# Hybrid attention and RWKV-7 layer: y products in the U half of a PSUM bank, four banks in turn, first RWKV step in the groups list

## The chip, the cores and the metric

The kernel runs on one core of a Trainium2 chip. The metric is device microseconds of one execution. The engines are named as in the profile: PE (TensorE matmul), PEld (its weight loads), DVE (VectorE), ACT (ScalarE), POOL (GpSimd) and SP (SyncE, which here only issues DMAs).

## What is computed

One transformer-like layer on 2048 latent tokens and 256 context tokens of width 1024. The reference, cut to the token mixer, which the change touches:

```python
q_l, k_l, v_l, rw_l = jnp.split(h_lat @ w_in, ATT_CUTS, axis=-1)
...
att_l = lax.map(lambda qb: gqa_attend(qb, k_all, v_all), q_blocks)      # 8 query heads, 2304 keys
...
for d, reverse in enumerate((False, True)):                              # RWKV-7, both directions, 8 heads
    s_c, yc = wkv7_scan(r_c, dc, kc, vr_c, ac, bc, s0, reverse, with_ctx_out)
    _, yl = wkv7_scan(r_l, dl, kl, vr_l, al, bl, s_c, reverse, True)
    y_l = yl if y_l is None else y_l + yl
rw_out_l = rwkv_output(y_l, r_l, kb_l, vr_l, g_l, r_k, lnx_g, lnx_b).astype(h_lat.dtype)
out_l = jnp.concatenate([att_l, rw_out_l], axis=-1) @ w_out
```

where one step of the scan is `S_t = S_{t-1} (diag(w_t) + a_t b_t^T) + v_t k_t^T ; y_t = S_t r_t`. Behind it come the output projection, a norm, and sixteen experts that each take their top 256 tokens.

## The kernel before

The layer runs in stages, one after the other: input projection (`inproj`), mixers (`mixers`), output projection (`outproj`), experts (`experts`). Only `mixers` is changed.

**Two kinds of work on one PE.** Attention runs in 32 units (a pair of heads by 256 queries), each of 9 groups of two key tiles. A group is four score matmuls (L871, L872) into tile `st`, two exponentials on ACT (L876) into `pt`, eight value matmuls (L897) into `po`, and two additions of `pt` to `acc` on POOL (L904) for the denominator. Ahead of a unit its queries are transposed (L823) and 20 products (L841) are each reduced to row maxima on DVE (L843). RWKV runs in 18 steps `m` (two pairs of heads, each a context step and 8 latent steps of 256 tokens, both directions at once). A step has these parts, each a generator: `elementwise` (the decay and rate products L1036, then a long run on ACT, DVE and POOL up to the tiles `AR` and `BK`), `lmats` and `trans` (products in chunks of 64, L1080, L1110, L1117), `inverse` (16x16 triangular inverses on DVE, sent through DRAM), `merges` (L1186), `chain` and, for the later half of a pair's steps, `post`.

**The chain** is the serial part: four quarters `c` per step, each carrying the state `S` on. A quarter does, in this order: 32 matmuls into `pa[:, 0]` (L1232, L1234), a copy to `xs` (L1237), 16 matmuls into `pa[:, 1]` (L1242, the U product), its two copies into `UV` (L1244), 16 matmuls back into `pa[:, 0]` (L1250), and, in a latent step, 32 y products (L1257, L1260). Then DVE forms `sn = pa[:, 0] + S` (L1263) and the new `S` (L1265), ACT copies `S` to `SB` (L1269), and y goes to `yt` by two ACT copies (L1274, first four latent steps of a pair) or two DVE additions (L1276, the last four). Tile `pa` (named `cha`) is 128x512 float32, a whole PSUM bank, and there is one of it. The y products have a bank of their own, tile `chy`.

**PSUM** has eight banks: three taken in turn under the name `bk` for everything else (each `bank()` call waits until the tile three calls back has been read), two for `st`, one each for `po`, `cha` and `chy`.

**Order on PE.** All matmuls of the mixers are put in one fixed order by `weave`, while the program is built. Each generator yields steps with a due time, a PE mode, a PE cost, the work that must follow (`seq`), work that nobody waits for (`bg`), what it needs, and how many `bk` banks it takes. `weave` keeps modelled clocks of PE, ACT, DVE and POOL and a list of when banks come free, and takes the step with the smallest key:

```python
key = due * self.STEP_NS + 30.0 * wait + cost      # STEP_NS = 66e3, cost 5000 where the PE mode changes
```

A step with mode `None` has no PE work and doesn't move the model's PE clock. PE then executes strictly in that order; the other engines' queues are ordered by the framework's scheduler.

**Before the list.** `first()` of attention (transposed keys, unit 0's queries and maxima) and `first()` of RWKV run ahead of `weave`. RWKV's `first()` loads the weights of two head pairs and then does `elementwise(0, i, 0)` and `lmats(0, i, 0)` for both `i`; the streams `elementwises` and `lmatss` start with step 1 and only name step 0 as made. The tile `wl` in pool `rwpre` exists once, and the raw weights (`headw`), the `wl` loads (L1023) and the tile `kd` of `elementwise` all take it in turn.

Of the kernel before, what the change touches and what calls it, by code (L numbers as in the profile page):

```python
# [10 lines left out]
F32 = mybir.dt.float32  # L11
# [24 lines left out]
class Layer:  # L36
# [614 lines left out]
    @staticmethod  # L651
    def step(due, mode=None, pe=0, seq=(), bg=(), need=(), bk=0):

        return due, mode, pe, seq, bg, need, bk
# [3 lines left out]
    def weave(self, streams):  # L660


        t = dict(PE=0.0, ACT=0.0, DVE=0.0, POOL=0.0)
        made, banks, shape = {}, [0.0] * 3, None

        def run(at, work):
            ends = []
            for e, ns in work:
                if e == "dma":
                    at += ns  # L670
                else:
                    t[e] = max(t[e], t["PE"]) + ns
                    at = max(t[e], at + ns + 100)
                ends.append(at)
            return at, ends

        live = []

        def forward(s):

            for x in s["gen"]:
                if isinstance(x, str):
                    late = x.endswith("+")
                    made[x.rstrip("+")] = max(s["ready"], t["POOL"] + 100) if late else s["ready"]
                else:
                    s["next"] = x
                    return
            live.remove(s)

        for g in streams:  # L690
            s = dict(gen=g, ready=0.0)
            live.append(s)
        for s in live[:]:
            forward(s)
        while live:
            best = None
            for s in live:
                due, mode, pe, seq, bg, need, bk = s["next"]
                if any(n not in made for n in need):
                    continue  # L700
                at = max([s["ready"]] + [made[n] for n in need] + banks[:bk])
                if mode is None:
                    wait, cost = max(at - t["PE"], 0.0), 0.0
                else:
                    wait, cost = max(at - t["PE"], 0.0), 0.0 if mode == shape else 5000.0
                key = due * self.STEP_NS + 30.0 * wait + cost
                if best is None or key < best[0]:
                    best = key, s, at
            _, s, at = best
            due, mode, pe, seq, bg, need, bk = s["next"]  # L710
            if mode is None:
                end = at = max(at, t["PE"])
                end, ends = run(at, seq)
            else:
                t["PE"] = max(t["PE"], at) + (0 if mode == shape else 170) + pe
                shape = mode
                end, ends = run(t["PE"] + 150, seq)
                if bk:
                    del banks[:bk]
                    banks += [ends[min(bk, len(ends)) - 1] if ends else end] * bk  # L720
            s["ready"] = end
            run(t["PE"], bg)
            forward(s)
# [16 lines left out]
    def attention(self, pools, pp):  # L740


        tc, nc = self.tc, self.nc
# [10 lines left out]
        step = self.step  # L754
# [5 lines left out]
            return RW * n / (NU * NG)  # L760

        def bank():
            return pp.tile([128, 512], F32, name="bk", bufs=3)

        def kprep(j, both):

# [171 lines left out]
    def rwkv(self, pools, pp):  # L938


        tc, nc, I = self.tc, self.nc, self.I
        CD = math.exp(-0.5)
        NB = 4
        NW = T // 256
        low, res, pre, lms, wk = (pools[n] for n in ("rwlow", "rwres", "rwpre", "rwlm", "rwwork"))
        ident = self.ident
        step = self.step
# [1 line left out]
        mean, hmean, gd, td, ypart = self.mean, self.hmean, self.gd, self.td, self.ypart  # L949

        def bank(shape):
            return pp.tile(shape, F32, name="bk", bufs=3)

        UPS, GW = {}, {}

        def headw(hp):
            hs = slice(128 * hp, 128 * hp + 128)
            raw = pre.tile([128, 2, 2, 256], F32, name="wl")[:, :, :, 0:128]
            for x, n in enumerate(("decay_up", "iclr_up")):
                for h in range(2):  # L960
                    nc.sync.dma_start(raw[cr(h), x], I[n][0, :, :, hs].rearrange("d k n -> k d n"))
            ups = UPS[hp] = [res.tile([128, 2, 2, 128], F32R, name=f"ups{a}", bufs=2) for a in range(2)]
            self.split(ups[0], ups[1], raw)
# [11 lines left out]
        def mats(t, h):  # L975

            return bass.AP(tensor=t.tensor, offset=t.offset + h * 8 * 4160, ap=[[64, 64], [4160, 8], [1, 64]])

        def cr(h):

            return slice(64 * h, 64 * h + 64)

        def tr(h):

            return slice(64 - 64 * h, 128 - 64 * h)
# [9 lines left out]
        N = len(steps)  # L995
        W, J, G, ST = {}, {}, {}, {}

        SB = [res.tile([128, 2, 2, 2, 64], F32, name=f"SB{j}") for j in range(2)]
        NS = [0]

        def hp_of(m, i):
            return 2 * steps[m][0] + i
# [70 lines left out]
        def products(m, i, x):  # L1073

            AR, BK = J[m]["AR"][:, i], G[m, i]["BK"]
            ps = [bank([128, 8, 64]) for _ in range(2)]
            for c in range(8):
                for h in range(2):
                    lhs = BK[cr(h), c].rearrange("p s j -> p (s j)")[:, 64 * h:64 * h + 128]
                    nc.tensor.matmul(ps[h][:, c], lhs, AR[cr(h), c, x], start=True, stop=True)  # L1080
            L = lms.tile([128, 8, 2, 64], F32, name="LR" if x else "LA", bufs=2 if x else 4)
            for h in range(2):
                nc.vector.tensor_mul(L[:, :, h], ps[h],
                                     mask[:, 64 * x:64 * x + 64].unsqueeze(1).to_broadcast([128, 8, 64]))
            return L

        def lmats(m, i, d0):
            yield step(d0, "r", 900, [("DVE", 687), ("DVE", 687)], bk=2, need=[f"E{m}.{i}"])
            LA = G[m, i]["LA"] = products(m, i, 0)
            for h in range(2):  # L1090
                nc.sync.dma_start(mats(gd[(2 * m + i) % NB], h), LA[tr(h), :, h])
            yield f"L{m}.{i}"
# [111 lines left out]
        def chain(m, d0):  # L1204
            pair, s = steps[m]
            lat = s >= 0
            yt = None
            for c in range(4):
                d1 = d0 + c * 0.1
# [14 lines left out]
                                                  .rearrange("i p n -> p i n"))  # L1224
                S = ST[0]
                pa = pp.tile([128, 2, 2, 2, 64], F32, name="cha", bufs=1)
                py = pp.tile([128, 2, 2, 64], F32, name="chy", bufs=1)
                for i in range(2):
                    for d in range(2):
                        q = 4 * d + c  # L1230
# [11 lines left out]
                            nc.tensor.matmul(pa[tr(h), 1, i, d], Y[i][tr(h), 4 * d + c], xs[tr(h), i, d], start=True, stop=True)  # L1242
                for h in range(2):
                    nc.scalar.copy(UV[tr(h), :, c::4, h], pa[tr(h), 1])  # L1244
                yield step(d1 + 0.06, "c", 1300 if lat else 430, [("DVE", 420), ("DVE", 420)],
                           [("ACT", 1150)] if lat else [])
                for i in range(2):
                    for d in range(2):
                        for h in range(2):
# [13 lines left out]
                nc.vector.tensor_add(sn, pa[:, 0], S)  # L1263
                ST[0] = wk.tile([128, 2, 2, 64], F32, name="S", bufs=2)
                nc.vector.tensor_mul(ST[0], sn, P[:, :, c::4].unsqueeze(3).to_broadcast([128, 2, 2, 64]))  # L1265
                if lat or c == 3:
                    NS[0] += 1
                    for h in range(2):
                        nc.scalar.copy(SB[NS[0] % 2][cr(h), h], ST[0][cr(h)])  # L1269
                if lat:  # L1270
                    for d in range(2):
                        dst = (yt[:, :, 1][:, :, ::-1] if d else yt[:, :, 0])[:, :, c * 64:(c + 1) * 64]
                        if s < NW // 2:
                            nc.scalar.copy(dst, py[:, :, d])  # L1274
                        else:
                            nc.vector.tensor_add(dst, py[:, :, d], dst)  # L1276
            if lat and s < NW // 2:
                for d, w in enumerate((s, NW - 1 - s)):
                    nc.sync.dma_start(ypart[2 * pair:2 * pair + 2, :, w * 256:w * 256 + 256].rearrange("i p n -> p i n"),
                                      yt[:, :, d])  # L1280
# [86 lines left out]
        def first():  # L1367
            for b in SB:
                nc.gpsimd.memset(b, 0.0)
            for i in range(2):  # L1370
                headw(i)
                load(0, i)
            for i in range(2):
                yield from elementwise(0, i, 0)
                yield from lmats(0, i, 0)


        OFF = 0.5

        def elementwises():  # L1380
            yield "E0.0"
            yield "E0.1"
            for m in range(1, N):
                for i in range(2):
                    yield from elementwise(m, i, m - 1.5 + OFF + 0.15 * i)
                    if m + 1 < N and steps[m + 1][1] < 0:
                        headw(hp_of(m + 1, i))

        def lmatss():
            yield "L0.0"  # L1390
            yield "L0.1"
            for m in range(1, N):
                for i in range(2):
                    yield from lmats(m, i, m - 1.25 + OFF + 0.15 * i)

# [705 lines left out]
```

## Time and profile before

| | |
|---|---|
| Time, median of 3 runs | 3928.14 us (3928.07 to 3928.42) |
| The profiled execution's own time | 3935.49 us |
| Its span | 3933.8 us |
| PE busy | 3555.9 us, 90% of the span |
| DVE, ACT, POOL busy | 66%, 44%, 37% |
| Mean granted TensorE clock | 0.944 of full speed |
| Mixers, about 669 to 2445 us | PE busy 1542.95 of the 1700 us from 740 to 2440 |

The busy time of PE is pipelined matmul time at whatever clock was granted, so a stretch at half clock looks busier than it is productive. An idle time in a row names what ended it, which for a tile taken in turn can be an instruction that the waiting one does not read.

### The profile page before, as it was taken

The numbers are of one execution on the slowest core, as the hardware profiler recorded it, in microseconds if no ns is written. First come the engines' busy times: TensorE is split into PE (matmuls) and PEld (weight loads), VectorE is DVE, ScalarE is ACT, GpSimd is POOL, SyncE is SP. The second block draws the span as 40 slices with busy tenths as digits, with TensorE's granted clock in tenths as the row PEclk, the third lists the DMA queues.
The fourth block names the chain that finished last, engine by engine and source line by source line (L and its number), as shares of the span: only waits on it lengthen the run. The fifth ranks groups of instructions, "written<-read, shape, count | busy, mean of one in ns | idle before, by whom it ended". The sixth has DMA issues, their size and how long they took to land. (4 is left out here: it accounts for less than half of the span.)

```text
span 3933.8 us, 83032 instructions
## 1 busy us (share of the span) xinstructions
PE 3555.9 (90%) x34103; PEld 2979.2 (76%) x34103; DVE 2603.1 (66%) x4413; ACT 1718.9 (44%) x3255; POOL 1445.9 (37%) x1326
## 2 busy tenths in 40 slices
PE   7999898699998988999998898993999999999986
PEld 6888897566666666666666666993999999999976
DVE  5665655567666776766666776787555556655688
ACT  4544353344444433444444434552444444444443
POOL 3332312456655554566655542333101101011025
PEclk8999999799999998999999998996999999999998
DMA  7756443223332323332232323434566667666675
GB/s 235 235 186 191 144 153 133 71 57 75 71 81 64 81 82 84 101 86 76 65 75 74 96 56 124 151 140 135 186 211 208 216 201 214 211 210 215 206 270 171
DMA packets 635533, 554.78 MB, mean 141 GB/s; under 512 B 264112, under 2 KB 584144, under 8 KB 635152
## 3 DMA queue, kind: packets, MB, share of 16 engines
q1 hardware_dynamic: 622672, 505.94, 41.9%
q0 software_dynamic: 12480, 43.52, 4.7%
q8 instruction: 268, 4.39, 0.4%
q14 instruction: 113, 0.93, 0.1%
HBM read 428.28 MB, written 121.03 MB: 140 GB/s over the span
## 5 line engine op out<-in xcount | busy, mean ns | idle before, releaser
L904 POOL TENSOR_TENSOR acc<-acc,pt 128x512 f32<-128x512 f32 x496 | 661.7, 1334 | 386.4 <-ACT pt L876 361.3
L48 DVE TENSOR_TENSOR wl<-wf,wh 128x1024 fp32r<-128x1024 f32 x434 | 532.7, 1253 | 264.3 <-ACT wh L43 264.3
L1979 PE MATMUL gu<-xh,wl 128*128 128x256 f32 x2048 | 584.6, 286 | 21.9 <-DVE wl L48 21.9
L1979 PE MATMUL gu<-xl,wh 128*128 128x256 f32 x2048 | 583.0, 285 | 0.0
L1979 PE MATMUL gu<-xh,wh 128*128 128x256 f32 x2048 | 581.8, 284 | 0.0
L43 ACT CAST wh<-wf 128x1024 fp32r<-128x1024 f32 x434 | 440.7, 1047 | 317.6 <-issue 106.1
L843 DVE TENSOR_REDUCE mx<-bk 128x1 f32<-128x512 f32 (+1 forms) x640 | 378.1, 629 | 183.7 <-PE bk L841 182.6
L876 ACT ACTIVATE pt<-st 128x512 f32<-128x512 f32 x576 | 317.1, 596 | 388.6 <-PE st L872 358.2
L1979 PEld LDWEIGHTS gu<-xh,wl 128*128 128x128 f32 x2048 | 390.3, 191 | 23.7 <-DVE wl L48 23.7
L1979 PEld LDWEIGHTS gu<-xh,wh 128*128 128x128 f32 x2048 | 391.3, 191 | 0.6
L1979 PEld LDWEIGHTS gu<-xl,wh 128*128 128x128 f32 x2048 | 389.4, 190 | 0.6
L897 PE MATMUL po<-pt,vt 128*64 128x256 f32 x2304 | 329.0, 412 | 0.9 <-ACT pt L876 0.9
L2023 POOL DMA_INDIRECT acc<-ysb,idx x30 | 48.3, 1611 | 675.0 <-DVE ysb L2020 589.3
L460 PE MATMUL mm<-hTh,wh 128*128 128x256 f32 x968 | 281.5, 291 | 4.4 <-POOL raw L479 2.2
L460 PE MATMUL mm<-hTl,wh 128*128 128x256 f32 x968 | 278.8, 288 | 1.2 <-DVE hTl L48 1.2
L460 PE MATMUL mm<-hTh,wl 128*128 128x256 f32 x968 | 276.2, 285 | 0.0
L841 PE MATMUL bk<-k,qs 128*128 128x512 f32 (+1 forms) x640 | 235.1, 436 | 37.3 <-DVE mx L843 23.2
L871 PE MATMUL st<-qs,k 128*128 128x512 f32 x576 | 253.8, 441 | 2.1 <-ACT pt L876 1.1
L872 PE MATMUL st<-q,kl 65*128 65x512 f32 x576 | 240.2, 417 | 12.9 <-DMA q<-mr 12.9
L897 PEld LDWEIGHTS po<-pt,vt 128*64 128x64 f32 x2304 | 150.1, 144 | 111.8 <-issue 59.8
L460 PEld LDWEIGHTS mm<-hTh,wh 128*128 128x128 f32 x968 | 186.5, 193 | 12.8 <-issue 7.9
L841 PEld LDWEIGHTS bk<-k,qs 128*128 128x128 f32 x640 | 108.6, 195 | 111.6 <-DVE mx L843 37.9
(431 smaller groups left out, 8401.4 us busy)
## 6 DMA issues: line engine op xcount, KB each, us to landing
wf<-in_exp_w_gate_dram SPq DMA_DIRECT2D x64, 1024.0 KB
wf<-in_exp_w_up_dram SPq DMA_DIRECT2D x64, 1024.0 KB
wf<-in_exp_w_down_dram SPq DMA_DIRECT2D x64, 1024.0 KB
win<-rkl SPq DMA_DIRECT2D x64, 512.0 KB
wf<-in_w_in_dram SPq DMA_DIRECT2D x30, 1024.0 KB
wf<-in_w_ada_dram SPq DMA_DIRECT2D x20, 1024.0 KB
wl<-wll SPq DMA_DIRECT2D x64, 256.0 KB
pwin<-rkl SPq DMA_DIRECT2D x32, 384.0 KB
```

Source lines behind the costliest of these rows:

```text
L43: nc.scalar.copy(hi, src)
L48: nc.vector.tensor_sub(lo, src, hi)
L460: mm = nc.tensor.matmul(ps[:, c], a[:, k, cs], b[:, k], start=m == 0, stop=m == 3 * KD - 1)
L841: nc.tensor.matmul(ps[:, :n], qs[:, hh, i * 128:(i + 1) * 128], K2[j][:, c * 512:c * 512 + n], start=True, stop=True)
L843: nc.vector.reduce_max(mx[:, hh * 2 + i, c:c + 1], ps[:, :n], axis=AX.X)
L871: nc.tensor.matmul(st, K2[j][:, ksl], qs, start=True, stop=False)
L872: nc.tensor.matmul(st, KL[j][:, ksl], q2, start=False, stop=True)
L876: nc.scalar.activation(pt, st, AF.Exp, scale=0.125)
L897: nc.tensor.matmul(po[hh * 64:(hh + 1) * 64], VT[j][:, kt], pt[:, hh], start=kt == 0, stop=kt == KT - 1)
L904: add(acc, acc, pt)
L1979: mm = nc.tensor.matmul(ps[:, i], a[:, k, 128 * c:128 * c + 128], b[:, k], start=n == 0, stop=n == 3 * KD - 1)
L2023: nc.gpsimd.indirect_dma_start(out=self.acc, in_=y[h], in_offset=None, compute_op=ALU.add, out_offset=bass.IndirectOffsetOnAxis(ap=idx[h], ...
```

## The change

Four edits, all in `mixers`. The y products go into `pa[:, 1]`, where U stood, and tile `chy` is gone. `bk` tiles are taken four in turn instead of three, in the kernel and in the planner's model. The planner's step for the last third of a quarter now counts y's two evictions as work that must follow (on ACT or DVE), and their place in the program moves ahead of the `SB` copies. And `first()` of RWKV ends after its loads (`return` ahead of a `yield`, so it stays a generator): `elementwise(0, i)` and `lmats(0, i)` are now in the streams, with the due times that the formulas give for m = 0.

```diff
-        made, banks, shape = {}, [0.0] * 3, None
+        made, banks, shape = {}, [0.0] * 4, None
...
-            return pp.tile([128, 512], F32, name="bk", bufs=3)
+            return pp.tile([128, 512], F32, name="bk", bufs=4)
...
-            return pp.tile(shape, F32, name="bk", bufs=3)
+            return pp.tile(shape, F32, name="bk", bufs=4)
...
                 pa = pp.tile([128, 2, 2, 2, 64], F32, name="cha", bufs=1)
-                py = pp.tile([128, 2, 2, 64], F32, name="chy", bufs=1)
+                py = pa[:, 1]
...
-                yield step(d1 + 0.06, "c", 1300 if lat else 430, [("DVE", 420), ("DVE", 420)],
-                           [("ACT", 1150)] if lat else [])
+                yield step(d1 + 0.06, "c", 1300 if lat else 430,
+                           [("DVE", 420), ("DVE", 420)] + [("ACT" if s < NW // 2 else "DVE", 300)] * (2 if lat else 0),
+                           [("ACT", 560)] if lat else [])
...
-                if lat or c == 3:
-                    NS[0] += 1
-                    for h in range(2):
-                        nc.scalar.copy(SB[NS[0] % 2][cr(h), h], ST[0][cr(h)])
                 if lat:
                     for d in range(2):
                         dst = (yt[:, :, 1][:, :, ::-1] if d else yt[:, :, 0])[:, :, c * 64:(c + 1) * 64]
...
                             nc.vector.tensor_add(dst, py[:, :, d], dst)
+                if lat or c == 3:
+                    NS[0] += 1
+                    for h in range(2):
+                        nc.scalar.copy(SB[NS[0] % 2][cr(h), h], ST[0][cr(h)])
...
-            for i in range(2):
-                yield from elementwise(0, i, 0)
-                yield from lmats(0, i, 0)
+            return
+            yield
...
         def elementwises():
-            yield "E0.0"
-            yield "E0.1"
-            for m in range(1, N):
+            for m in range(N):
                 for i in range(2):
                     yield from elementwise(m, i, m - 1.5 + OFF + 0.15 * i)
...
         def lmatss():
-            yield "L0.0"
-            yield "L0.1"
-            for m in range(1, N):
+            for m in range(N):
                 for i in range(2):
                     yield from lmats(m, i, m - 1.25 + OFF + 0.15 * i)
```

## Rows read from the trace of the kernel before

**Rows 1.** The page: busy time of PE, and the granted clock in 40 slices.

```profile
PE 3555.9 (90%) x34103; PEld 2979.2 (76%) x34103; DVE 2603.1 (66%) x4413; ACT 1718.9 (44%) x3255; POOL 1445.9 (37%) x1326
...
PEclk8999999799999998999999998996999999999998
```

**Rows 2.** Stretches: length, busy PE, PEld, DVE, ACT, POOL, granted clock, DMA share, GB/s.

```profile
680.00:700.00 20.00, 6.26 (x42) 5.81 (x42) 7.62 (x7) 3.44 (x7) 6.02 (x7) 0.50 0.30 98
700.00:720.00 20.00, 10.66 (x69) 8.18 (x68) 8.51 (x10) 5.88 (x13) 4.63 (x5) 0.50 0.30 63
...
740.00:2440.00 1700.00, 1542.95 (x18917) 1108.32 (x18919) 1152.43 (x2011) 731.42 (x1617) 937.22 (x781) 0.94 0.31 77
```

**Rows 3.** Timeline of PE, 669 to 717: start, length, instruction, idle before and what ended it.

```profile
684.11 2.05 PE L1036 MATMUL bk<-wl,ups 128*128 128x256 f32 x8 [13.84 <-DMA wl<-wlc]
695.05 3.68 PE L1080 MATMUL bk<-AR,BK 64*128 64x64 f32 x32 [8.89 <-DVE BK L1066]
699.46 2.26 PE L1036 MATMUL bk<-wl,ups 128*128 128x256 f32 x8 [0.74 <-DMA wl<-wlc]
710.78 3.77 PE L1080 MATMUL bk<-AR,BK 64*128 64x64 f32 x32 [9.06 <-DVE BK L1066]
```

**Rows 4.** Timeline of POOL in the same stretch, step 0, head pair 0.

```profile
687.84 1.71 POOL L1061 TENSOR_TENSOR wl<-wl,win 128x512 f32<-128x512 f32 x1 [3.82 <-DVE wl L1058]
...
691.50 1.18 POOL L1059 TENSOR_TENSOR AR<-win,P 128x512 f32<-128x512 f32 x1
...
692.94 1.42 POOL L1067 TENSOR_TENSOR BK<-wl,tw 64x512 f32<-64x512 f32 x1
```

**Rows 5.** Waits of PE, 740 to 2440: us in total, times, longest us.

```profile
PE bk L841 <- DVE mx L843: 19.8, 21, 2.0
...
PE bk L1186 <- DVE mx L843: 11.7, 8, 3.2
PE cha L1232 <- DVE S L1265: 10.3, 7, 2.7
...
PE bk L1339 <- DVE mx L843: 5.6, 3, 3.4
...
PE bk L919 <- ACT BT L1112: 2.0, 1, 2.0
```

**Rows 6.** Groups by line, 740 to 2440: busy us, mean ns of one, idle before.

```profile
L904 POOL TENSOR_TENSOR acc<-acc,pt 128x512 f32<-128x512 f32 x489 | 650.7, 1331 | 369.9 <-ACT pt L876 345.0
L843 DVE TENSOR_REDUCE mx<-bk 128x1 f32<-128x512 f32 x612 | 361.8, 629 | 177.7 <-PE bk L841 176.8
```

**Rows 7.** Timeline of PE around the longest wait for a bank.

```profile
1266.62 0.71 PE L841 MATMUL bk<-k,qs 128*128 128x512 f32 x2
1270.73 0.60 PE L1339 MATMUL bk<-ident,pvt 128*4 128x128 f32 x4 [3.41 <-DVE mx L843]
```

**Rows 8.** Timeline, all engines: end of one chain quarter and start of the next.

```profile
2384.88 0.42 DVE L1263 TENSOR_TENSOR sn<-cha,S 128x256 f32<-128x256 f32 x1 [1.15 <-ACT UV L1244]
...
2385.34 0.43 DVE L1265 TENSOR_TENSOR S<-sn,Pend 128x256 f32<-128x256 f32 x1
2385.43 0.29 PE L1260 MATMUL chy<-LR,UV 128*64 128x64 f32 x4
...
2385.76 0.49 DVE L1276 TENSOR_TENSOR yt<-chy,yt 128x128 f32<-128x128 f32 x2
...
2386.09 0.39 PE L871 MATMUL st<-qs,k 128*128 128x512 f32 x1
...
2386.80 0.40 PE L872 MATMUL st<-q,kl 65*128 65x512 f32 x1
...
2387.13 0.27 PE L1232 MATMUL cha<-S,AR 64*64 64x64 f32 x2
```

**Rows 9.** Timeline of PE at the end of the mixers.

```profile
2439.27 1.95 PE L897 MATMUL po<-pt,vt 128*64 128x256 f32 x16
...
2445.83 0.39 PE L1512 MATMUL mm<-woh,mh 128*128 128x256 f32 x1 [3.68 <-ACT mh L43]
```

## The prediction, made before the changed kernel ran

> **What bounds the kernel now.** I read the page first, for the engines and the clock over the span, then stretches, then PE's timeline and PE's waits in the mixers. PE is busy 90% of the span and no other engine is over 66% [rows 1], so time is won only where PE stands idle or runs at the lower of its two clock levels (1.2 and 2.4 GHz). Only the mixers change, so the question is how much of either lies there. From 740 to 2440 PE is busy 1543 of 1700 us at a mean granted clock of 0.94 [rows 2]: 157 us idle and, by the clock, about 0.06 x 1700 = 102 us lost to the lower level. Just ahead of that, from 680 to 720, the clock is 0.50 and PE is busy 17 of 40 us [rows 2]. The timeline shows why [rows 3]: PE waits 13.84 us for the first load of `wl`, then 8.89, 0.74 and 9.06 us while step 0 of RWKV goes through ACT, DVE and POOL, and no attention work stands between those matmuls in PE's order. When the list of groups is through, the output projection starts within 5 us of the last value matmuls [rows 9]; what the mixers gain arrives there whole, and the stages behind it are not touched.
>
> **The change part by part.**
>
> *Step 0 in the list.* It removes no instruction and adds none; it lets the planner put attention groups between step 0's matmuls. The first 13.84 us stay: the planner reckons 2.3 us for the `wl` load, places one attention group ahead of L1036 as now, and the real load is as late as before. The other three waits are 8.89 + 0.74 + 9.06 = 18.7 us [rows 3]. Is there work to fill them? A group costs PE about 1.1 us of scores (2386.09 to 2387.20 [rows 8]) and 0.98 us of values (1.95 for two groups [rows 9]), so nine groups would do. POOL must add each group in two pieces of 1.33 us [rows 6], 24 us for nine, beside step 0's own POOL work of twice 1.71 + 1.18 + 1.42 = 8.6 us [rows 4]: together 32.6 us in a stretch of 33, so it just fits, and unit 1's twenty products are there as well. But step 0 is due 1.0 to 0.6 ahead of attention, and in the key a whole step is worth 66,000 / 30 = 2.2 us of wait, so PE is kept idle rather than given a group wherever the planned wait is shorter. Four PE steps remain after the first load; I take 1.2 us lost at each, so 14 of the 18.7 us are won. With the gaps filled PE should also leave 0.50 earlier: the four matmul rows hold 11.8 us of work at the lower level [rows 3], 5.9 at the full one, and I take 5. Together **-19 us**; bounds 0 and -25. Step 0's ACT, DVE and POOL work, which now runs alone, mixes with exponentials, maxima and additions; PE has attention to do meanwhile, so I cost that at nothing, and if that cover is short the 14 shrink. The queues' loads stay in their order: `wl` still waits for the raw weights in the same tile, and the SP work queued behind it is unit 1's queries, loaded before.
>
> *A fourth bank.* A wait for a bank shows as a wait on an instruction whose result the waiting one doesn't read: the transposes of `pvt` wait 3.41 us on a row maximum [rows 7]. Of PE's waits, twelve kinds of 19.8 down to 2.0 us are such (the first and the last of them in [rows 5]), 51 waits and 58.8 us in all. With four in turn a tile needs the reader four calls back, one reader earlier, and the commonest reader takes 0.63 us [rows 6]. So each wait loses at most about 0.63 us, 51 x 0.63 = 32 us. Part passes to the next tile, since DVE must read them all anyway, and the planner spends some of the new room on a denser order. I take -20 us. Clock: 102 us are lost beside 157 us idle, so 20 us fewer idle would in proportion be 13; idle of under a microsecond may not move the clock, so I take -5. Together **-25 us**. Bounds: all 58.8 us and the proportional clock (38) gone, -97; on the other side a new order that meets worse waits, which I bound by the three longest kinds growing by a quarter (37.1 / 4, [rows 5]), +9.
>
> *y in U's half.* The y products need `UV`, which is read out of that half first, so they wait for nothing new. Two later steps may. First, DVE's `sn` starts at 2384.88, while y products run until 2385.72 [rows 8]: it reads the state half of the bank into whose other half PE is now writing. If that is kept apart, `sn` starts 0.84 us later. The Trainium skill, in "PSUM — Partial Sum Buffer", section "PSUM bank collisions raise a hardware error", says two engines may not touch one bank and quadrant at once whichever columns they use; no run here shows a collision, but by it the 0.84 us would be paid in every latent quarter. Second, `pa` exists once, so the next quarter's L1232 now waits for y's evictions, 0.49 us on DVE behind `S` [rows 8]; on ACT they run beside `sn` and `S` and cost nothing more. So `S` and the bank are free up to 0.84 + 0.49 = 1.33 us later in half of the 64 latent quarters (the DVE half) and 0.84 in the other. In that row `S` is done at 2385.77 and L1232 starts at 2387.13, after maxima and a score group: 1.36 us of cover, just enough. Uncovered it would be 32 x 1.33 + 32 x 0.84 = 69 us; with other work placed between, nothing. The planner already began `sn` after the y products and now counts both evictions, so it places that work; today seven chain starts wait, 10.3 us [rows 5]. I take nearly a doubling, **+8 us**; bounds 0 and 69. The `SB` copies slip 0.43 to 0.49 us; their reader is the next y product, most of a quarter later.
>
> **Sum.** -19 - 25 + 8 = -36 us. The profiled execution took 3935.5 us (span 3933.8 and 1.7 around it), 7.4 above the median of the runs. So 3899.5 for such an execution, and 3928.1 - 36 = **3892 us** against the median.
>
> **Rivals.**
> - *B, the banks are worth much more:* nearly all 58.8 us go and the lower clock with them. For: the waits come in runs on a DVE that is idle 178 us waiting for PE's products [rows 6], so it has room. Against: an order made with four banks uses four. -19 - 65 + 8 gives about 3852.
> - *C, the banks give nothing:* DVE's queue is the limit where they wait (3.41 us is five reductions of 0.63, not one [rows 6, 7]). Then -19 + 8: about 3917.
> - *D, no change:* the change doesn't do what it says at the start. PE's fixed order is made on a model in which step 0 is ready within 2.3 us, so its matmuls again stand close together and PE waits in order; and what the banks give, the chain takes. Against: the model's own latency from L1036 to `BK` is over 10 us, five times what the key lets PE idle. About 3928.
> - *E, slower, the chain becomes the bound:* its place is L1232 at the head of every latent quarter. For: `sn` behind the y products and one bank for everything; a cover of 1.36 us is already only just enough [rows 8]; and RWKV starts behind attention now, so the key prefers a waiting chain to a ready group. It decides if more than two thirds of the 69 us stay uncovered, that is, more than the 44 us won elsewhere. The whole 69 gives 3928 - 44 + 69 = 3953. The rule of the Trainium skill named above is what would make the 0.84 us certain; its being covered is a matter of order alone. Against: 65 of 72 quarters don't wait today [rows 5].
>
> **How the numbers follow.** Forecast (3872 to 3909) 0.50, B 0.14, C 0.14, D 0.10, E 0.12. The range 3855 to 3932 leaves out most of E and the far half of B, about 0.2. A measurement here can tell about 0.2%, 8 us, from no change: faster is below 3920, which the forecast, B and C are: 0.78; same 0.10; slower 0.12.
>
> **What would show it.** Right: between 684 and 717 score and value matmuls (L871, L872, L897) stand between L1036 and L1080, the two waits on `BK` are under 3 us together, and the clock is back before 700; the first wait of some 14 us is still there. Waits of PE on L843 through `bk` fall from 37 us to some 20, with fewer half-clock stretches. `sn` begins after the last y product, and the waits of L1232 grow to under 20 us, on L1265, L1276 or L1274. Wrong: waits of L1232 above 45 us, or waits for banks that are as long as now in a changed order. If the mixers' end moves by the sum while the stages behind keep their length, the sum was right for its reasons.

## The result, and the profile after

The changed kernel takes **3883.35 us**, median of 4 runs (3878.33 to 3888.95), against 3928.11 (3926.57 to 3928.42): a ratio of **0.9882 [0.9866, 0.9898]**, 44.8 us less by the medians. The forecast was 3892, faster. The profiled execution took 3881.74 us, its span is 3880.0, 53.8 less than the span before; so the two traces differ by some 9 us more than the medians. From line 1245 on, the changed kernel's lines stand one to two higher up to the `SB` copies (y products L1258 and L1261, `sn` L1264, `S` L1266, y's evictions L1271 and L1273, `SB` L1277); the output projection is L1508.

The page of the changed kernel, against [rows 1]: PE's busy time falls by 35 us for the same 34103 matmuls, while the span falls by 54.

```profile
PE 3521.1 (91%) x34103; PEld 2969.3 (77%) x34103; DVE 2584.3 (67%) x4413; ACT 1714.7 (44%) x3255; POOL 1446.5 (37%) x1326
...
PEclk8999998799999999899999998996999999999988
```

Stretches, with the columns of [rows 2]; the last two rows end where the output projection's first matmul starts and where the span ends. First the changed kernel:

```profile
660.00:680.00 20.00, 7.31 (x22) 4.63 (x23) 7.16 (x13) 12.74 (x25) 2.29 (x4) 0.50 0.68 214
680.00:700.00 20.00, 15.40 (x48) 9.28 (x47) 13.23 (x24) 5.71 (x13) 3.98 (x3) 0.66 0.03 7
700.00:720.00 20.00, 16.05 (x115) 10.89 (x115) 14.07 (x21) 11.31 (x23) 16.16 (x13) 0.91 0.27 73
...
735.00:745.00 10.00, 2.52 (x13) 0.66 (x13) 6.38 (x13) 0.69 (x2) 6.39 (x7) 0.64 0.03 9
745.00:760.00 15.00, 2.66 (x34) 2.29 (x34) 5.99 (x13) 0.62 (x1) 1.55 (x1) 0.50 0.55 120
...
640.00:760.00 120.00, 75.73 (x480) 54.93 (x478) 73.21 (x147) 45.86 (x98) 48.26 (x47) 0.74 0.34 94
760.00:2387.94 1627.94, 1489.74 (x18837) 1088.01 (x18836) 1127.56 (x2013) 724.99 (x1614) 920.38 (x771) 0.95 0.32 80
2387.90:3880.00 1492.10, 1380.37 (x10186) 1292.46 (x10186) 997.19 (x1561) 662.08 (x998) 282.41 (x137) 0.95 0.61 197
```

The same stretches of the kernel before:

```profile
735.00:745.00 10.00, 5.99 (x31) 3.19 (x32) 8.80 (x12) 3.36 (x6) 9.64 (x9) 0.84 0.45 75
745.00:760.00 15.00, 14.70 (x244) 12.56 (x246) 7.47 (x12) 1.08 (x2) 4.28 (x4) 0.73 0.31 75
...
640.00:760.00 120.00, 78.03 (x679) 65.69 (x679) 68.78 (x144) 34.91 (x80) 42.23 (x47) 0.73 0.37 104
760.00:2445.83 1685.83, 1529.07 (x18686) 1095.94 (x18682) 1145.50 (x2016) 731.50 (x1619) 929.77 (x777) 0.94 0.31 77
2445.80:3933.80 1488.00, 1374.66 (x10186) 1287.66 (x10186) 998.41 (x1564) 662.22 (x998) 283.27 (x137) 0.96 0.61 197
```

Two things are to be read here. The mixers end 57.9 us earlier (2445.83 to 2387.94) and the stages behind take 4.1 us more, at a clock lower by 0.01. And **the opening gave nothing**: from 640 to 760, where the first RWKV step lies, PE was busy for 75.73 us against 78.03, at about the same clock (0.74 and 0.73). Another mix of work was done in it: 72 value matmuls (L897) started there where 54 did, but 34 products of the merges (L1186) where 224 did, so attention is ahead and RWKV behind. From 700 to 720 it was busier than before, as forecast (16.05 against 10.66), but from 660 to 680 the clock is at 0.50, the lower level, and from 735 to 760 PE worked 5.2 of 25 us where it had worked 20.7.

PE's timeline of the changed kernel in the opening, against [rows 3]:

```profile
656.66 0.28 PE L422 MATMUL mm<-wh,hTl 128*128 128x256 f32 x1
656.78 0.60 PE L788 MATMUL bk<-ident,kt 128*128 128x128 f32 x4
660.50 1.08 PE L788 MATMUL bk<-ident,kt 128*128 128x128 f32 x4 [3.12 <-DVE qko L410]
...
693.79 1.91 PE L1036 MATMUL bk<-wl,ups 128*128 128x256 f32 x8
...
707.44 2.00 PE L1080 MATMUL bk<-AR,BK 64*128 64x64 f32 x30 [1.42 <-POOL BK L1067]
710.20 2.24 PE L1036 MATMUL bk<-wl,ups 128*128 128x256 f32 x8 [0.76 <-DMA wl<-wlc]
...
741.68 1.12 PE L919 MATMUL bk<-acc,ones 128*64 128x256 f32 x4 [5.65 <-POOL acc L904]
...
756.91 0.47 PE L1186 MATMUL bk<-Z,LA 64*64 64x64 f32 x2 [12.55 <-DMA Z<-td]
```

Step 0's waits are filled (1.42 and 0.76 us where there were 8.89, 0.74 and 9.06). But L1036 comes 9.7 us later than before, without a wait of its own, and behind step 0 stand two new waits of 5.65 and 12.55 us.

PE's waits of the changed kernel from 740 to 2395, against [rows 5].

```profile
PE cha L1232 <- DVE yt L1273: 9.5, 6, 3.0
...
PE cha L1232 <- DVE S L1266: 9.0, 8, 3.7
...
PE bk L841 <- DVE mx L843: 7.1, 7, 2.9
```

Beside the three kinds in [rows 5], 37.1 us together, the kernel before has two smaller ones on L843 through `bk`:

```profile
PE bk L1080 <- DVE mx L843: 3.0, 2, 1.8
```

With these two (the other is 0.3 us) and two more of 0.6 us after, the waits on row maxima are down from 40.4 us to 8.3. L1232, the head of a quarter, has two kinds of wait where it had one, 18.5 us for 10.3.

### The profile page after: what moved, and what is told of

Its sections match the earlier page's. It is cut to its first block, busy times and chain, and to the rows that moved or that the text cites. A ratio compares the mean times of both kernels' runs of the same rounds, so it can differ in the third digit from the quotient of the medians.

```text
span 3880.0 us, 83041 instructions
## 1 busy us (share of the span) xinstructions
PE 3521.1 (91%) x34103; PEld 2969.3 (77%) x34103; DVE 2584.3 (67%) x4413; ACT 1714.7 (44%) x3255; POOL 1446.5 (37%) x1326
## 5 line engine op out<-in xcount | busy, mean ns | idle before, releaser
L843 DVE TENSOR_REDUCE mx<-bk 128x1 f32<-128x512 f32 (+1 forms) x640 | 377.9, 627 | 154.8 <-PE bk L841 153.9
L897 PE MATMUL po<-pt,vt 128*64 128x256 f32 x2304 | 320.2, 403 | 1.6 <-ACT pt L876 1.3
L841 PE MATMUL bk<-k,qs 128*128 128x512 f32 (+1 forms) x640 | 230.7, 440 | 16.5 <-DVE mx L843 7.3
L897 PEld LDWEIGHTS po<-pt,vt 128*64 128x64 f32 x2304 | 145.6, 140 | 104.1 <-issue 45.6
L460 PEld LDWEIGHTS mm<-hTl,wh 128*128 128x128 f32 x968 | 186.7, 193 | 6.2 <-issue 4.1
```

The lines of the kernel that those rows point to most:

```text
L460: mm = nc.tensor.matmul(ps[:, c], a[:, k, cs], b[:, k], start=m == 0, stop=m == 3 * KD - 1)
L841: nc.tensor.matmul(ps[:, :n], qs[:, hh, i * 128:(i + 1) * 128], K2[j][:, c * 512:c * 512 + n], start=True, stop=True)
L843: nc.vector.reduce_max(mx[:, hh * 2 + i, c:c + 1], ps[:, :n], axis=AX.X)
L897: nc.tensor.matmul(po[hh * 64:(hh + 1) * 64], VT[j][:, kt], pt[:, hh], start=kt == 0, stop=kt == KT - 1)
```

## The experiments

Chips differ, so ratios are compared, each against the kernel before on the same chip; where two ratios are subtracted, 0.001 is 3.9 us and both intervals count. The time of before was 3928.92 us beside e1 to e4, 3936.77 beside e5 to e8 and 3936.29 beside e9 to e11. All eleven kernels compute the whole layer.

**e1, the list alone.** The kernel before with the last of the four edits only.

> Step 0 of RWKV goes into the list; y keeps its own bank and three banks are taken in turn. By the prediction's sum this alone gives -19 us: about 3909, with the two waits of 9 us on BK between 684 and 717 gone. The rival that the start gains nothing (attention gets ahead and the planner then lets PE wait for RWKV) gives 3925 to 3930. If the whole change owes its 45 us to the start, this is near 3883.

Measured: 3919.94 us, 0.9969 [0.9955, 0.9983], 12 us less by the ratio (9 by the medians), of the 19 forecast. PE's timeline of e1:

```profile
702.88 2.25 PE L1036 MATMUL bk<-wl,ups 128*128 128x256 f32 x8
715.43 2.13 PE L1080 MATMUL bk<-AR,BK 64*128 64x64 f32 x32
...
738.71 0.37 PE L849 MATMUL bk<-ident,nm 128*4 128x128 f32 x1 [4.33 <-DVE nm L846]
...
747.32 2.51 PE L1186 MATMUL bk<-Z,LA 64*64 64x64 f32 x32 [4.63 <-DMA Z<-td]
```

The second pair's matmuls no longer wait at all, and some of it comes back as waits of 4.33 and 4.63 us around 740. The first wait for `wl` stayed, as the prediction had it: 14.05 us ahead of L1036 at 685.96.

**e2, y alone**, and **e3, y and banks.** e2 has y in `pa[:, 1]`, the planner's count of y's evictions and the new place of the `SB` copies, with three banks and step 0 ahead of the list. e3 is e2 with the fourth bank, so the change without the list.

> Only the y products go into U's half, with the planner's count of the evictions and their place ahead of the SB copies; three banks in turn, the freed bank stays empty. By the sum this costs 8 us: about 3936, with waits of L1232 near 20 us. If the longer quarter is uncovered (rival E) up to 69 us: above 3970. If sn behind the y products is fully covered, 3928 or a little less, since a new order also moves other waits.

> The change without its last edit: y in U's half and four banks, step 0 still ahead of the list. By the sum 8 - 25 = -17: about 3911. Theory P: the fourth bank is one of those in which the input projection still accumulates, so attention's transposed keys and unit 0's products, which before ran between its last matmuls, now wait for its end; then the start is about 10 to 20 us later than before and step 0's waits of 18.7 us come on top, and the time is 19 to 25 us above the changed kernel: 3902 to 3908, with the first product of step 0 (L1036) near 693 instead of 684.

Measured: e2 3936.01 us, 1.0014 [0.9995, 1.0034]; e3 3889.33, **0.9898 [0.9868, 0.9929]**. So y costs about 6 us, not told from none, and the fourth bank is worth 1.0014 - 0.9898, **46 us**, give or take 14 by the two intervals. y's part holds three edits at once (the half, the count and the place of the `SB` copies). For e3 both forecasts were too high. L1036 starts at 691.25 and L1080 still waits 6.93 and 8.85 us for `BK`, as theory P had it; but instead of 19 to 25 us this costs 6 to 13 against the changed kernel by the ratios (0.9882, and 0.9866 in e11). The stretch from 760 to the first matmul of the output projection, e2 and then e3:

```profile
760.00:2450.65 1690.65, 1523.88 (x18715) 1099.93 (x18710) 1135.26 (x2019) 728.87 (x1619) 931.69 (x778) 0.94 0.31 77
```
```profile
760.00:2401.96 1641.96, 1504.35 (x18848) 1094.96 (x18847) 1129.73 (x2023) 726.75 (x1619) 925.29 (x776) 0.94 0.32 79
```

Of the 48.7 us between them 29.2 are idle time (166.8 to 137.6) and 19.5 are busy time for much the same work. Busy time is the time in which at least one matmul is in the records, and a single record is hardly shorter (value matmuls L897 405 ns in the mean in both, L1080 288 and 280, most products of the merges L1186 224 and 228), so the records also lie closer together. Part is the clock: its mean over the whole execution is 0.941 in e2 and 0.944 in e3, which by their spans (3942.9 and 3890.7 us) is, as an estimate, some 15 us less lost to the lower level, all stages counted. How the 19.5 divide is not shown. Waits of e2:

```profile
PE cha L1232 <- DVE yt L1273: 18.4, 10, 5.5
PE bk L841 <- DVE mx L843: 14.8, 17, 2.0
PE cha L1232 <- DVE S L1266: 8.9, 6, 3.0
PE bk L1186 <- DVE mx L843: 8.5, 10, 4.1
...
PE bk L1186 <- DVE mA L1194: 5.2, 5, 1.9
```

And of e3, in the same stretch:

```profile
PE bk L1186 <- DVE mA L1194: 15.4, 9, 2.9
PE cha L1232 <- DVE S L1266: 14.8, 7, 4.7
...
PE cha L1232 <- DVE yt L1273: 7.2, 4, 2.8
...
PE bk L841 <- DVE mx L843: 4.0, 6, 1.5
```

All waits on L843 through `bk`, the small kinds with them, fall from 31.7 us in 40 waits to 4.6 in 7, and the kind on L1186 is gone. A part comes back as a wait of L1186 for its own operand `mA`, 5.2 to 15.4 us. The head of the chain waits 27.3 us in e2 where about 20 were expected, and 22.0 in e3.

**e5 and e6, the bank on the chip or in the plan.** The changed kernel, with the planner left at three banks in e5, and with the tiles left at three in e6.

```diff
-        made, banks, shape = {}, [0.0] * 4, None      # e5
+        made, banks, shape = {}, [0.0] * 3, None
...
-  name="bk", bufs=4)                                  # e6, both places
+  name="bk", bufs=3)
```

> The changed kernel, but the planner still reckons with three banks while the kernel takes four in turn. Theory H (one more bank of slack on the chip for an order made for three): most of the banks' 46 us stay, 3880 to 3895, and the waits on row maxima are nearly gone. Theory O (the gain is the planner's other order): it is lost, 3915 to 3930.

> The reverse: the planner reckons with four banks, the kernel takes three in turn; the prologue of attention stays inside the input projection, which is worth 13 us by the run with the pools. Theory H: an order that leans on a fourth bank which isn't there waits more than before: 3925 to 3960, waits on L843 through bk above 40 us. Theory O: 3870 to 3890.

Measured: e5 3891.73 us, **0.9886 [0.9860, 0.9911]**, all of the change's gain as far as the intervals tell; e6 3947.13, **1.0031 [1.0018, 1.0044]**, none of it. PE's waits for banks, in e5 and then e6:

```profile
PE bk L841 <- DVE mx L843: 2.9, 2, 2.4
```
```profile
PE bk L841 <- DVE LR L1083: 16.5, 10, 3.3
...
PE bk L841 <- DVE mx L843: 11.4, 11, 2.7
PE bk L841 <- DVE LA L1083: 9.0, 13, 1.8
```

The bank pays as slack while the kernel runs, theory H. The order that is planned with it adds nothing that these runs can tell, and the same order without the bank is slower than the kernel before. One sign of H was missed: e6 waits 26.1 us on L843 through `bk`, all kinds together, and not over 40; another 25.5 are the two kinds on L1083.

**e4, the prologue's place.** The wait on `qko` at 660.50, ahead of attention's transposes, suggested that the fourth `bk` tile lies where the input projection's `mm` tiles were, so that attention's preparation has to wait for the end of that stage. e4 is the changed kernel with another order of three pools there, in which `bk` takes the `kk` bank:

```diff
             ptp = es.enter_context(tc.tile_pool(name="p1tp", bufs=3, space=PSUM, reuse_waits="tile"))
+            pkk = es.enter_context(tc.tile_pool(name="p1kk", bufs=1, space=PSUM, reuse_waits="tile"))
             pmm = es.enter_context(tc.tile_pool(name="p1mm", bufs=3, space=PSUM, reuse_waits="tile"))
-            pkk = es.enter_context(tc.tile_pool(name="p1kk", bufs=1, space=PSUM, reuse_waits="tile"))
```

> The changed kernel with one line moved in the input projection: its pool kk (one bank, last used well ahead of the end) is allocated ahead of mm, so that the fourth bank in turn is kk's instead of one of mm's. Theory P: transposed keys and unit 0's products run between the last matmuls of the input projection again, L1036 comes near 684 instead of 694, and the time falls by 10 to 25 us: 3858 to 3873. If which bank is the fourth doesn't matter, 3883 as the changed kernel.

Measured: 3869.78 us, 0.9848 [0.9821, 0.9876]. The 20 products of unit 0 (count; shortest, median and longest ns; first and last start), in the kernel before, the changed one and e4:

```profile
L841 PE MATMUL bk<-k,qs x20: 279/391/502, 518.6 to 530.1; 128*128 128x512 f32 x16, 128*128 128x256 f32 x4
```
```profile
L841 PE MATMUL bk<-k,qs x20: 382/628/796, 677.1 to 687.4; 128*128 128x512 f32 x16, 128*128 128x256 f32 x4
```
```profile
L841 PE MATMUL bk<-k,qs x20: 279/391/502, 622.4 to 633.5; 128*128 128x512 f32 x16, 128*128 128x256 f32 x4
```

Before, they ran inside the input projection at 391 ns; in the changed kernel they run behind it, alone and at 628 ns. The granted clock was 1.00 from 518 to 531 before, and is 0.66 from 677 to 688 in the changed kernel. In e4 they are inside again, and L1036 starts where it did before:

```profile
684.12 2.28 PE L1036 MATMUL bk<-wl,ups 128*128 128x256 f32 x8 [14.44 <-DMA wl<-wlc]
```

**e10, e4 without the list**, and **e11, the change once more**, on another chip.

> The run with the pools without the last edit: y in U's half, four banks, the prologue of attention inside the input projection, step 0 ahead of the list. The edit alone was worth 12 us on three banks, and 6 us on top of the others with the prologue outside. If the prologue's place is what made the difference, it is worth 12 here: 12 us above the run with the pools. If the hole at 735 to 760 is what eats it whatever the prologue does, 4 to 8 us above.

> The changed kernel as it is, beside the two others on the same chip: 1.2% under the kernel before, as measured first.

Measured: e10 3886.67 us, 0.9862 [0.9842, 0.9882]; e11 3888.64, 0.9866 [0.9844, 0.9887]. With the pools in order the bank is worth 1.0014 - 0.9862, 60 us, give or take 11. The place of the prologue costs 9.7 us by the start of L1036, and by ratios 7 to 14 (e4 against the change's 0.9866 and 0.9882; e10 against e3); the intervals overlap. The list on top of the bank gives 6 to 13 us (e3 against the change's two ratios) or 6 (e10 against e4), intervals overlapping too: only e1 shows it clear of none. The 6 of e10 would be the second of its two expectations, 12 the first; the intervals do not decide between them.

**e7 and e8, the planner's delays.** e4's first load of `wl` still leaves PE idle for 14.44 us, and the waits around 740 remain. The model reckons 2300 ns for that load and 5000 for each trip of the inverse. From the end of `LA` to the first work on `X` the changed kernel takes up to 9.3 us (727.02 to 736.33); from the last sum into `T` (ends 750.80) to L1186, 6.1. The first of these is not the trip alone, since DVE works on `BK` (L1064) from 734.68 until then; and for the second e8 puts in 9 us, more than the 6.1 that this trace shows. e7 is e4 with the load's delay changed for step 0, e8 is e7 with the trips' delays changed for step 0. Nothing but the order of matmuls follows from these.

```diff
-            yield step(d0, None, 0, [("dma", 2300)], ...                                  # e7
+            yield step(d0, None, 0, [("dma", 16e3 if m + i == 0 else 2300)], ...
...
-            yield step(d0 - 0.1, None, 0, [("dma", 5000)], ...                            # e8
+            yield step(d0 - 0.1, None, 0, [("dma", 5000 if m else 10e3)], ...
...
-            yield step(d0 + 6 * q, None, 0, [("ACT", 625), ("dma", 5000)],
+            yield step(d0 + 6 * q, None, 0, [("ACT", 625), ("dma", 5000 if m else 9e3)],
```

> The run with the pools (3870), and the planner's model of the very first wl load is 16 us instead of 2.3, as the traces show it. If PE's wait of 14 us ahead of L1036 can be filled with attention groups, 8 to 14 us less: 3856 to 3862. If attention then runs further ahead of its additions on POOL and the time is given back at the hole between 735 and 760 (theory Q), 3865 to 3872, with that hole longer.

> As the one before, and the planner's two DRAM trips of step 0's inverse are 10 and 9 us instead of 5 and 5, as the traces show them. If the hole between 735 and 760 is PE waiting for Z in an order made for a shorter trip, it shrinks by 8 to 15 us: 5 to 15 us below the run before. If the hole is DVE and POOL being behind (theory Q), no difference within 5 us.

Measured: e7 3863.26 us, 0.9816 [0.9789, 0.9844], not told from e4, and between its two expectations; e8 3844.91, **0.9779 [0.9756, 0.9802]**, faster than both kernels and 18 us under e7. The stretches that they fill, e7 and then e8:

```profile
660.00:680.00 20.00, 16.26 (x101) 13.14 (x100) 13.84 (x43) 7.79 (x19) 7.46 (x11) 0.86 0.17 57
...
740.00:760.00 20.00, 9.17 (x158) 8.66 (x159) 7.05 (x10) 0.62 (x1) 5.14 (x3) 0.57 0.36 66
```
```profile
740.00:760.00 20.00, 17.63 (x248) 13.91 (x247) 17.50 (x22) 6.24 (x12) 16.01 (x14) 0.74 0.55 110
```

In e8, L1186 starts at 754.03 with no wait. DVE and POOL are busy two and a half and three times as long in that stretch as in e7, so the hole was not theirs: PE had no other matmul in its order there. The hole also goes with the order made for four banks: with step 0 in the list but three banks in the plan, the longest wait for `Z` is 4.6 us in e5 and 4.63 in e1. Which of the two trips the model has most wrong was not tried alone.

**e9, the evictions uncounted.** The changed kernel with the old planner step for the last third of a quarter.

> The changed kernel with the planner's count of the last third of a quarter as before (y's evictions reckoned as work nobody waits for); y stays in U's half, the copies stay ahead of those of SB. If the count is what keeps the next quarter's products covered, the waits of L1232 grow from about 19 us to 35 or more and the time by 5 to 20 us: 3888 to 3903. If the planner's old estimate, which already begins sn after the y products, covers them, no change: 3880 to 3888.

Measured: 3905.89 us, 0.9922 [0.9905, 0.9938], against e11's 0.9866 on the same chip: the count is worth 22 us (17 by the medians). PE's waits of e9 (its lines are one lower):

```profile
PE cha L1232 <- DVE S L1265: 18.4, 10, 4.8
...
PE cha L1232 <- DVE yt L1272: 12.7, 8, 3.3
```

That is 31.1 us at the chain's head where the changed kernel has 18.5; 35 or more were expected.

## Why the prediction was right, and where its terms were not

The side and the range were right, in part by luck: the bank was taken too small by about 21 us and the list too large by about 13, two errors that partly cancel.

- **y in U's half, +8: right in mechanism, and in size as far as it was measured.** e2 gives +6 with an interval from -2 to +13. `sn` begins behind the last y product, and L1232 waits for y's evictions. All engines' timeline of the changed kernel:

```profile
2020.25 0.29 PE L1261 MATMUL cha<-LR,UV 128*64 128x64 f32 x4
...
2020.65 0.42 DVE L1264 TENSOR_TENSOR sn<-cha,S 128x256 f32<-128x256 f32 x1 [2.88 <-PE cha L1261]
...
2222.38 0.33 PE L1232 MATMUL cha<-S,AR 64*64 64x64 f32 x4 [1.29 <-DVE yt L1273]
```

  The last y product ends at 2020.54 and `sn` starts at 2020.65, where [rows 8] has `sn` running beside the products. It holds for all 64 latent quarters: `sn` starts 0.05 to 4.41 us behind the last y product, where it started ahead of that product's end in 53 of them before. The Trainium skill, "PSUM — Partial Sum Buffer", section "PSUM bank collisions raise a hardware error", has it that a reader must stay off a bank and quadrant that PE writes, other columns or not. The trace agrees in order in all 64, 0.11 us apart here; whether chip or program would have minded an overlap, no run shows. L1232 waits 9.5 + 9.0 = 18.5 us, under the 20 named, but 27.3 in e2, where y stands alone: 17 us more than before for some 6 us of time, so other waits got shorter with the new order. Rival E needed over 44 us there, and fell. The planner's count of evictions holds these waits down (e9), but e9 without it has only 31.1 and is still faster than before.
- **The fourth bank, -25: the mis-sized term; it measured -46, and -60 with the prologue in its place.** Between e2 and e3 idle time fell by 29 us where 20 were taken, and 19.5 us of busy time went with it where 5 "of clock" were taken; the second is the larger miss. The reason for taking 5 and not 13, that short idle times may leave the clock alone, no run tests. Behind the 20 stands "each wait loses at most about 0.63 us". For the 40 waits on L843 in e2 that allows 25 us, and 27.1 went, those of up to 4.1 us on L1186 whole; the discount from 32 to 20 was too much rather than the limit far off. The objection to rival B, "an order made with four banks uses four", fell with e5 and e6: the time is as good with three in the plan. With the prologue in its place the bank comes near B's own figure, -65; without, it lies halfway between B's and mine. B's total was not reached for the next two reasons. How one bank removes several readings' worth of wait is not shown by a row.
- **Step 0 in the list, -19: half right.** Its first claim held: of 18.7 us 2.2 are left (1.42 and 0.76), so 16.5 went where 14 were taken. The step that failed is "I cost that at nothing", said of step 0's ACT, DVE and POOL work, which now mixes with attention's: the sum took it that a wait filled in the opening is time won, and did not follow the opening past 717. Attention put ahead runs into POOL's additions (5.65 us at L919) and into an inverse for which the order keeps too little work (12.55 us at L1186). e1 keeps 12 us of it, the change 6 to 13; e8 shows that the second of these waits was a matter of the planner's delays.
- **"The first 13.84 us stay": right in e1 (14.05), wrong in the change, for a reason that the sum does not have.** In the changed kernel the wait for `wl` is gone, since attention's preparation now stands there; but that had been free inside the input projection, and L1036 comes 9.7 us later. The edit of a `bufs` number moved work across a stage's border. This is a cost of the bank, and I named no work outside the mixers as its cover.
- **The stages behind** did not quite keep their length: 4.1 us longer at a clock of 0.95 for 0.96. The four runs of the changed kernel lie up to 10.6 us apart, so this is within what they differ by. That "what the mixers gain arrives there whole" held: the mixers end 57.9 us earlier and the span is 53.8 shorter.

So in ratios against before: +6 (y), -46 (bank, with the prologue's cost in it) and -6 (list) make -46; the forecast had +8, -25 and -19. That they add up proves nothing, since each is the step from one run to the next and the list's is what is left; by e11's ratio it would be -13.

## What to carry to other kernels

On an in-order engine with a fixed order, a further buffer in turn can be worth more than one reader's time for each visible wait (here 46 or 60 us where that gave 32), and it works as slack at run time, so try it on the chip whatever the planner says; but look at which earlier stage's buffer it takes over, for that stage's end may have been covering work. When a gap is filled by moving work ahead, follow that work to the next wait: a planner with too short a delay gives the gain back there, and longer delays for the first step were worth more (0.9848 to 0.9779, about 27 us) than the edit that they spoilt (12 us alone).

## What the hardware showed that was not expected

Fewer gaps went with less busy time. Between e2 and e3, 29 us fewer idle went with 19.5 us fewer busy for much the same work, at a mean granted clock of 0.944 for 0.941; what else than the clock shortens it stays open. In the opening of the changed kernel, the 20 products that took a median of 391 ns inside the input projection, at the full clock, took 628 ns behind it, at a mean granted clock of 0.66. PE had been idle for most of 660 to 680, where the clock was at 0.50, the lower level.
